# Low parts of 24 weight tiles by accumulating transfers, norms by logarithm and exponential, and one PSUM pool

## The chip, the cores and the metric

The kernel runs on one core of a Trainium2 chip. The metric is the device time of one execution in microseconds (us), and the figure of a kernel is the median of its runs. The engines are called as in the profile: PE (TensorE, matrix products), DVE (VectorE), ACT (ScalarE), POOL (GpSimd) and SP (SyncE, which issues the transfers). PSUM, the memory that PE writes its products to, has eight banks.

## The reference

Two layers of an encoder run over 1024 prompt tokens and 32 sample tokens that share all weights, in fp32. Each layer is

```
x <- LN(alpha * x + mixer(x))          # in-projection, mixers, output projection w_out (1024 x 1024)
x <- LN(alpha * x + SwiGLU(x))         # (silu(x @ w1) * (x @ w3)) @ w2, hidden width 2816
x <- x + (p[i] @ W_ple) * sigmoid(x @ W_gate)
LN(x) = (x - mean) * rsqrt(var + 1e-5) * g + b
```

The mixers are pooling and a gated convolution in layer 0, and a spatial gate and a state space scan in layer 1. Nothing of them is touched by the change.

## The kernel before, in words

**Operands in two parts.** A matrix product in fp32 precision is made of three products of a reduced type (fp32r): the high part of the weight with the high part of the activation, the low part of the weight with the high part, and the high part of the weight with the low one (lines 314 to 316). So each weight tile is split: a transfer on SP's queue brings it into a buffer `raw` (there are 2), ACT copies it with rounding into the high part (line 93), and DVE subtracts the high part from `raw` to make the low part (line 94). The pairs (`w`) have 4 places. A tile is 128 x 1024 in the projections (a "unit") and 128 x 512 in most of the SwiGLU. `Weights` runs 4 tiles ahead of the products that use them, so that loads and splits are issued in the middle of other work.

**The order.** The tokens are worked in three pieces c of 384, 384 and 288 columns in the projections, and in two halves of 528 in the SwiGLU. The matrix products of the SwiGLU use a fast scheme of seven block products (and, for some blocks, a second level of seven inside them) instead of eight; their results are added on DVE into the areas `s_all` and `c_all` (the tile names of the profile). The instructions are first recorded, then a scheduler puts them in each engine's order; it knows the dependences and durations of its own model, and the order on an engine is then fixed.

**Stages of a layer.** The mixer, the output projection with its norm, the first tiles of `w1_` and `w3_` (`f` = 0 and 1, as units), the rest of the up products (`up`, lines 1236 and 1153), the down products (`final`, line 1448), the second norm, and the embedding.

**Up and final.** `up` works in a PSUM pool with three tiles q of two banks and two tiles of one bank, `ia` and `ib`. `within` (called for the second level) makes seven block products in `ia` and `ib`: `one` issues six matmuls of 264 columns into one bank, and `to` reads that bank with ACT (line 1162, a copy) or DVE (line 1164, an addition). Each product that follows in the same bank waits for the reader of the one before. `final` then opens another pool, with four tiles q.

**The norm.** Per piece, `norm` makes the mean and variance by a product with ones (`ms`), then 1/sqrt(var) in steps that are put among other work by `defer`: a root on ACT (line 1685), a reciprocal on DVE (line 1690), a square on ACT (line 1691) and one step of refinement (lines 1697 to 1703). Between them, `minus` subtracts the mean from two of eight slices at a time (line 1673). `pieces` then scales (line 1709 on DVE, line 1711 on ACT) and splits the result into high parts (line 411, ACT) and low parts (line 412, DVE), two slices at a time, four times. The first tiles of `w1_` and `w3_` on piece 0 need these parts.

Of the kernel before, what the change touches and what calls it, by code (L numbers as in the profile page):

```python
# [9 lines left out]
AF = mybir.ActivationFunctionType  # L10
# [44 lines left out]
class Weights:  # L55
# [35 lines left out]
    def split(self, t, x):  # L91
# [2 lines left out]
        self.nc.vector.tensor_tensor(lo, x, hi.bitcast(F32), op=ALU.subtract)  # L94
        return hi, lo

    def sub(self, a, b, op=ALU.subtract):
        t = self.temp(a.shape[1])
        self.nc.vector.tensor_tensor(t, a, b, op=op)  # L99
        return t  # L100

    def _make(self, order):
        for kind, key, src in order:
            if kind == "steps":
                yield from src()
            elif kind == "unit":
                raw = self.raw(src)
                yield key, 2, self.split(self.place()[:, :, :src.shape[1]], raw)
            elif kind == "set":
                yield from self._set(key, *src)  # L110
            elif kind == "22":
                yield key, 1, self.split(self.half(), self.raw(src[1][:, 512:1024]))
            else:

                r0, r1 = (self.raw(v) for v in src)
                a11, a12, a21, a22 = (r[:, h * 512:(h + 1) * 512] for r in (r0, r1) for h in range(2))
                own = lambda x: (key, 1, self.split(self.half(), x))
                if kind != "sums":
                    yield own(a11)
                    yield own(a12)  # L120
                s1 = self.sub(a21, a22, ALU.add)
                s2 = self.sub(s1, a11)
                if kind == "own":
                    yield own(self.sub(a12, s2))
                    continue
                yield own(s2)
                if kind == "all":
                    yield own(s1)
                yield own(self.sub(a11, a21))
                if kind == "sums":  # L130
                    yield own(s1)
                    continue
                yield own(self.sub(a12, s2))
                yield own(a22)
# [150 lines left out]
class Kernel:  # L285
# [50 lines left out]
    def build(self):  # L336
        nc, tc, a = self.nc, self.tc, self.a
        with ExitStack() as ctx:
# [44 lines left out]
            for layer in range(2):  # L383
                if layer == 0:
                    self.layer0_mixer(self.x, xraw)
                    mp.close()
                else:
                    self.layer1_mixer(self.x)
                with ExitStack() as stack:
                    self.hp = stack.enter_context(tc.tile_pool(name=f"h{layer}", bufs=1, reuse_waits="tile"))  # L390
                    self.w.temps, self.w.temp_bufs = self.hp, 5
                    self.tail(layer)
                    self.tp = stack.enter_context(tc.tile_pool(name=f"t{layer}", bufs=1, reuse_waits="tile"))
                    with tc.tile_pool(name=f"psu{layer}", bufs=1, space=PSUM, reuse_waits="tile") as self.psum:
                        self.psum_bufs = {"q": 3, "ia": 1, "ib": 1}
                        self.up(layer)
                    self.psum = stack.enter_context(
                        tc.tile_pool(name=f"psb{layer}", bufs=1, space=PSUM, reuse_waits="tile")
                    )
                    self.psum_bufs = {"q": 4}  # L400
                    self.final(layer)
                    self.embed(layer)

# [736 lines left out]
    def within(self, layer, j, g):  # L1140


        nc, q, d, x = self.nc, TH // 2, self.sh, self.inside[j]
        m, t = {2: (0, 0), 4: (1, 0)}[j]
        (w,) = self.w.get(("in", layer, g, j))

        def bank(tag):
            return self.bank(tag)[:, :q]

        def one(ps, i, add):  # L1150
            for k in range(2):
                for c, (p, r) in enumerate(((0, 0), (1, 0), (0, 1))):
                    nc.tensor.matmul(  # L1153
                        ps, w[i][p][:, k * P:(k + 1) * P], x[i][r][:, k, :],
                        start=not add and k == 0 and c == 0, stop=k == 1 and c == 2, skip_group_check=add,
                    )
            self.passed(6 * q)

        def to(a, b, ps, new=False):
            o = d[a][:, m, t * TH + b * q:t * TH + (b + 1) * q]  # L1160
            if new:
                nc.scalar.activation(o, ps, AF.Copy)
            else:
                nc.vector.tensor_tensor(o, o, ps, op=ALU.add)

        u = bank("ia")
        one(u, 1, False)
        to(0, 0, u)
        v = bank("ib")
        one(v, 2, False)  # L1170
        to(0, 0, v)
        yield
        v = bank("ib")
        one(v, 5, False)
        to(1, 1, v, True)
        one(u, 6, True)
        to(0, 1, u)
        yield
        one(v, 3, True)
        to(0, 1, v)  # L1180
        one(u, 7, True)
        to(1, 1, u)
        yield
        one(u, 4, True)
        to(1, 0, u, True)
        yield
# [460 lines left out]
    def norm(self, ln, c, S, acc, x, n, done, wait=LN_A, rows=None):  # L1647
# [33 lines left out]
        def second():  # L1681
            ps, cut = average(S[1])
            nc.vector.tensor_tensor(cut(var), ps, cut(tmp), op=ALU.subtract)
            nc.vector.tensor_scalar(out=var, in0=var, scalar1=0.0, scalar2=EPS, op0=ALU.max, op1=ALU.add)
            nc.scalar.activation(tmp, var, AF.Sqrt)
            minus(0)
            self.defer(LN_B, third)

        def third():
            nc.vector.reciprocal(inv, tmp)  # L1690
            nc.scalar.activation(tmp, inv, AF.Square)
            minus(2)
            self.defer(LN_B, fourth)

        def fourth():

            nc.vector.tensor_tensor(tmp, tmp, var, op=ALU.mult)
            nc.scalar.activation(tmp, tmp, AF.Copy, scale=-0.5, bias=1.5)
            minus(4)
            self.defer(LN_B, fifth)  # L1700

        def fifth():
            nc.vector.tensor_tensor(inv, inv, tmp, op=ALU.mult)
            pieces(0)

        def pieces(k):
            ks = slice(k, k + 2)
            z = acc[:, ks, :]
            nc.vector.tensor_tensor(z, z, inv.unsqueeze(1).to_broadcast([P, 2, n]), op=ALU.mult)
            for kk in (k, k + 1):  # L1710
                nc.scalar.activation(
                    acc[:, kk, :], acc[:, kk, :], AF.Identity,
                    scale=self.ln[:, ln, 0, kk:kk + 1], bias=self.ln[:, ln, 1, kk:kk + 1],
                )
            if k == 0:
                minus(6)
            self.split(x, ks, z)
            done[c] += 1
            if k + 2 < KD:
                self.defer(LN_D if rows else LN_C, lambda: pieces(k + 2))  # L1720
# [118 lines left out]
```

## Time and profile before

| | |
|---|---|
| median of 3 runs | 2300.8 us (2297.95 to 2302.07) |
| profiled execution, its time | 2300.83 us |
| its span in the trace | 2298.6 us |
| PE busy | 2270.4 us (99%) |
| DVE, ACT, POOL busy | 1736.9, 1060.7, 32.5 us |
| mean TensorE clock granted | 0.996 |

The span runs from the first to the last recorded instruction; about 2.2 us of the execution's time lie outside it. A matmul's row in the trace has a start and a modelled end; as they are pipelined, the distance from start to start is what one costs. A timeline row with "x24" covers 24 instructions that follow one another. A bracket at the end of a row tells how long the engine sat idle before it and what released it.

### The profile page before, as it was taken

How to read it: one execution, taken by the hardware profiler on the slowest of the kernel's cores; microseconds unless marked ns; L12 is line 12 of the kernel's file. 1: busy time of each engine (PE TensorE's matmuls, PEld its weight loads, DVE VectorE, ACT ScalarE, POOL GpSimd, SP SyncE). 2: the span in 40 equal slices, each digit the busy share in tenths (PEclk: the TensorE clock that was granted, in tenths of full speed). 3: DMA queues.
4: the chain of work that ended last, by engine and by line, in shares of the span. 5: the costliest groups of instructions: out<-in, count | busy, mean ns of one | idle time of the engine just before them, and what ended most of it. 6: DMA issues, size and time to landing. Idle time of an engine off the chain costs nothing.

```text
span 2298.6 us, 41143 instructions
## 1 busy us (share of the span) xinstructions
PE 2270.4 (99%) x17183; PEld 2236.8 (97%) x17183; DVE 1736.9 (76%) x2820; ACT 1060.7 (46%) x1783; POOL 32.5 (1%) x40
## 2 busy tenths in 40 slices
PE   9999999999999999999999999999999999999998
PEld 8999989999999999999999989999999999999998
DVE  8755798977776788896656774898977776888893
ACT  5432464434443443584542662464444443434581
POOL 0000000000000000000000120000000000000000
PEclk9999999999999999999999999999999999999999
DMA  4113133333334632034211222142332335631132
GB/s 143 55 56 113 56 140 102 107 116 107 107 116 162 255 121 70 28 102 139 84 38 57 102 67 72 38 154 96 123 111 94 112 107 204 256 106 42 47 105 91
DMA packets 96478, 241.46 MB, mean 105 GB/s; under 512 B 12092, under 2 KB 21508, under 8 KB 94244
## 3 DMA queue, kind: packets, MB, share of 16 engines
q1 hardware_dynamic: 95524, 238.15, 30.5%
q8 instruction: 134, 2.20, 0.4%
q10 hardware_dynamic: 768, 0.68, 0.1%
q14 instruction: 52, 0.43, 0.1%
HBM read 196.99 MB, written 41.81 MB: 104 GB/s over the span
## 4 chain that ended last, share of the span: by engine, by line
PE 88%; DVE 7%; DMA 2%; ACT 2%; issue 1%; SPq 0%; POOL 0%; POOLq 0%; ACTq 0%
PE q L1236 28%; PE q L1448 20%; PE q L1576 8%; PE mm L314 6%; PE mm L315 6%; PE mm L316 6%; PE ia L1153 4%; PE ib L1153 3%; PE q L1555 2%; DVE bf L99 1%; PE mm L727 1%; PE mm L728 1%; PE mm L729 1%; DVE w L94 1%; DMA raw<-w 1%; PE ms L863 1%
## 5 line engine op out<-in xcount | busy, mean ns | idle before, releaser
L1448 PE MATMUL q<-w 128*128 128x264 f32 x3696 | 459.1, 286 | 4.3 <-DVE c_all L1254 2.2
L1448 PEld LDWEIGHTS q<-w 128*128 128x128 f32 x3696 | 457.8, 189 | 4.9 <-ACT w L93 4.7
L93 ACT ACTIVATE w<-bf 128x512 fp32r<-128x512 f32 (+1 forms) x314 | 184.5, 626 | 190.2 <-issue 69.1
L94 DVE TENSOR_TENSOR w<-raw,w 128x512 fp32r<-128x512 f32 (+2 forms) x182 | 171.2, 946 | 97.7 <-ACT w L93 97.5
L94 DVE TENSOR_TENSOR w<-bf,w 128x512 fp32r<-128x512 f32 (+1 forms) x314 | 207.0, 687 | 37.7 <-ACT w L93 37.3
L93 ACT ACTIVATE w<-raw 128x512 fp32r<-128x512 f32 (+2 forms) x182 | 149.1, 828 | 163.9 <-PE mm L316 75.2
L314 PE MATMUL mm<-xhgate,w 128*128 128x384 f32 (+1 forms) x576 | 188.6, 327 | 4.7 <-ACT xhgate L411 4.7
L1236 PE MATMUL q<-xhin,w 128*128 128x264 f32 x1152 | 188.3, 285 | 0.6 <-ACT u L481 0.6
L316 PE MATMUL mm<-xlgate,w 128*128 128x384 f32 (+1 forms) x576 | 186.6, 325 | 0.8 <-DVE xlgate L412 0.8
L315 PE MATMUL mm<-xhgate,w 128*128 128x384 f32 (+1 forms) x576 | 187.1, 325 | 0.0
L1576 PE MATMUL q<-xhgate,w 128*128 128x264 f32 x1024 | 167.1, 285 | 0.0
L1236 PEld LDWEIGHTS q<-xhin,w 128*128 128x128 f32 x1152 | 159.5, 188 | 1.5 <-ACT u L481 0.8
L1576 PEld LDWEIGHTS q<-xhgate,w 128*128 128x128 f32 x1024 | 142.0, 188 | 0.3
L314 PE MATMUL mm<-xhin,w 128*128 128x384 f32 (+1 forms) x384 | 127.4, 332 | 7.8 <-ACT xhin L411 5.6
L315 PE MATMUL mm<-xhin,w 128*128 128x384 f32 (+1 forms) x384 | 126.1, 329 | 0.6 <-DVE w L94 0.6
L316 PE MATMUL mm<-xlin,w 128*128 128x384 f32 (+1 forms) x384 | 125.7, 329 | 0.1
L1236 PE MATMUL q<-xhgate,w 128*128 128x264 f32 x768 | 125.3, 285 | 0.3 <-ACT xhgate L1204 0.2
L1236 PE MATMUL q<-t3sum,w 128*128 128x264 f32 x960 | 124.3, 285 | 0.0
L1236 PE MATMUL q<-t1sum,w 128*128 128x264 f32 x960 | 124.0, 285 | 0.0
L1236 PE MATMUL q<-t2sum,w 128*128 128x264 f32 x960 | 123.6, 284 | 0.0
L1236 PEld LDWEIGHTS q<-t1sum,w 128*128 128x128 f32 x960 | 120.3, 189 | 0.0
L1236 PEld LDWEIGHTS q<-t3sum,w 128*128 128x128 f32 x960 | 120.0, 189 | 0.0
(431 smaller groups left out, 4801.9 us busy)
## 6 DMA issues: line engine op xcount, KB each, us to landing
raw<-w SPq DMA_DIRECT2D x116, 512.0 KB, 3.7
hidden<-c_all SPq DMA_DIRECT2D x72, 264.0 KB, 2.1
rawx<-w SPq DMA_DIRECT2D x64, 256.0 KB, 2.9
raw<-w_gate SPq DMA_DIRECT2D x32, 512.0 KB, 3.6
raw<-w_in SPq DMA_DIRECT2D x16, 512.0 KB, 3.8
raw<-w_out SPq DMA_DIRECT2D x16, 512.0 KB, 3.5
xhdown<-hidden SPq DMA_DIRECT2D x12, 528.0 KB, 13.6
resid<-stream SPq DMA_DIRECT2D x4, 1056.0 KB, 4.9
```

The costliest lines, as they stand in the source:

```text
L93: self.nc.scalar.activation(hi, x, AF.Copy)
L94: self.nc.vector.tensor_tensor(lo, x, hi.bitcast(F32), op=ALU.subtract)
L99: self.nc.vector.tensor_tensor(t, a, b, op=op)
L314: nc.tensor.matmul(ps, wh, xh, start=first, stop=False)
L315: nc.tensor.matmul(ps, wl, xh, start=False, stop=False)
L316: nc.tensor.matmul(ps, wh, xl, start=False, stop=last)
L727: nc.tensor.matmul(o, xh, hi[:, s], start=k == 0, stop=False)
L1153: nc.tensor.matmul(ps, w[i][p][:, k * P:(k + 1) * P], x[i][r][:, k, :], start=not add and k == 0 and c == 0, stop=k == 1 and c == 2, skip_ ...
L1236: nc.tensor.matmul(ps[:, a, :TH // 2], w[q][:, ks], x[r][:, k, a * TH // 2:(a + 1) * TH // 2], start=not add and k == 0 and j == 0, stop=k ...
L1448: nc.tensor.matmul(ps[m][:, a, :TH // 2], v[q][:, ms], x[r][:, a * TH // 2:(a + 1) * TH // 2], start=j == 0 and n == 0, stop=j == NG - 1 a ...
L1555: nc.tensor.matmul(ps[:, b, :TH // 2], w[q][:, o:o + P], pe[k][r][:, t * TH + b * TH // 2:t * TH + (b + 1) * TH // 2], start=k == 0 and i ...
L1576: nc.tensor.matmul(ps[:, b, :TH // 2], w[q][:, ks], token_half((self.xh, self.xl), k, t, b)[r], start=k == 0 and i == 0, stop=k == KD - 1 ...
```

## The change

Three edits. First, for the units of `w_out`, `w1_` and `w3_` (24 tiles: eight of `w_out` and four of `w1_`/`w3_` in each layer), `split_dma` takes the place of `split`: the high part is made as before, ACT writes minus the high part into the low part's place by a second copy, and a transfer issued by POOL adds `raw` to that place. No DVE instruction is left in it. Second, the norm makes 1/sqrt(var) as exp(-0.5 ln(var)) with three ACT instructions in a row; the reciprocal and one deferred step are gone, and the subtractions of the mean are spread over other steps. Third, the pool of `up` and that of `final` are one, with four tiles q; `within` takes one q and uses its two banks.

```diff
+    def split_dma(self, t, x):
+        hi, lo = t[:, 0, :], t[:, 1, :]
+        self.nc.scalar.activation(hi, x, AF.Copy)
+        self.nc.scalar.activation(lo, x, AF.Copy, scale=-1.0)
+        self.nc.gpsimd.dma_start(out=lo, in_=x, accum_op=ALU.add)
+        return hi, lo
...
                 raw = self.raw(src)
-                yield key, 2, self.split(self.place()[:, :, :src.shape[1]], raw)
+                split = self.split_dma if key[0].startswith(("w_out", "w1_", "w3_")) else self.split
+                yield key, 2, split(self.place()[:, :, :src.shape[1]], raw)
...
-                    with tc.tile_pool(name=f"psu{layer}", bufs=1, space=PSUM, reuse_waits="tile") as self.psum:
-                        self.psum_bufs = {"q": 3, "ia": 1, "ib": 1}
-                        self.up(layer)
                     self.psum = stack.enter_context(
                         tc.tile_pool(name=f"psb{layer}", bufs=1, space=PSUM, reuse_waits="tile")
                     )
                     self.psum_bufs = {"q": 4}
+                    self.up(layer)
                     self.final(layer)
...
-        u = bank("ia")
+        ps = self.quads()
+        u, v = (ps[:, a, :q] for a in range(2))
         one(u, 1, False)
         to(0, 0, u)
-        v = bank("ib")
         one(v, 2, False)
         to(0, 0, v)
         yield
-        v = bank("ib")
         one(v, 5, False)
...
-            nc.scalar.activation(tmp, var, AF.Sqrt)
+            nc.scalar.activation(tmp, var, AF.Ln)
+            nc.scalar.activation(inv, tmp, AF.Exp, scale=-0.5)
+            nc.scalar.activation(tmp, inv, AF.Square)
             minus(0)
             self.defer(LN_B, third)
 
         def third():
-            nc.vector.reciprocal(inv, tmp)
-            nc.scalar.activation(tmp, inv, AF.Square)
+
+            nc.vector.tensor_tensor(tmp, tmp, var, op=ALU.mult)
+            nc.scalar.activation(tmp, tmp, AF.Copy, scale=-0.5, bias=1.5)
             minus(2)
             self.defer(LN_B, fourth)
 
         def fourth():
-
-            nc.vector.tensor_tensor(tmp, tmp, var, op=ALU.mult)
-            nc.scalar.activation(tmp, tmp, AF.Copy, scale=-0.5, bias=1.5)
-            minus(4)
-            self.defer(LN_B, fifth)
-
-        def fifth():
             nc.vector.tensor_tensor(inv, inv, tmp, op=ALU.mult)
             pieces(0)
...
-            if k == 0:
-                minus(6)
+            if k < 4:
+                minus(k + 4)
```

The scheduler makes new orders of this. Three places follow; the number behind an underscore tells buffers apart, and a bracket names what an instruction waits for (DMASW is the completion of a transfer issued by POOL).

**PE, third unit of the output projection of layer 0** (`mm48` and `mm49` are two output tiles of piece 0, `w83` the unit). Before:

```order
L314 MATMUL mm48_2062<-xhin_63,w83_1988 128x384 [waits Activation_49]
L314 MATMUL mm49_2076<-xhin_63,w83_1988 128x384
L315 MATMUL mm48_2062<-xhin_63,w83_1988 128x384 [waits DVE_49]
L316 MATMUL mm48_2062<-xlin_64,w83_1988 128x384
```

Now:

```order
L323 MATMUL mm50_2096<-xhin_63,w85_1996 128x384 [waits DVE_49,Activation_49]
L323 MATMUL mm51_2110<-xhin_63,w85_1996 128x384 [waits DVE_49]
L323 MATMUL mm52_2124<-xhin_63,w79_1843 128x384 [waits DVE_49]
L324 MATMUL mm52_2124<-xhin_63,w79_1843 128x384
L325 MATMUL mm52_2124<-xlin_64,w79_1843 128x384
...
L323 MATMUL mm53_2138<-xhin_63,w79_1843 128x384 [waits DVE_49]
L324 MATMUL mm48_2068<-xhin_63,w83_1990 128x384 [waits DMASW2_49]
L325 MATMUL mm48_2068<-xlin_64,w83_1990 128x384
```

Work on the fourth unit (`w85`) and on the first one again (`w79`, for piece 1) now stands between the third unit's high product and its low one, which waits for a transfer of POOL instead of DVE.

**PE, one second-level block in `up`** (six matmuls make one product of `within`). Before:

```order
L1153 MATMUL ia136_4512<-xhin_63,w194_4358 128x264 [waits Activation_49]
L1153 MATMUL ia136_4512<-xhin_63,w194_4358 128x264
...
L1153 MATMUL ib137_4520<-xhin_63,w194_4358 128x264 x2
L1153 MATMUL ib137_4520<-xlin_64,w194_4358 128x264
L1236 MATMUL q138_4535<-t1sum0_3226,w197_4441 128x264 [waits DVE_49]
...
L1153 MATMUL ib139_4561<-inner0_3945,w195_4361 128x264 [waits DVE_49]
L1153 MATMUL ib139_4561<-inner0_3945,w195_4361 128x264 x5
L1153 MATMUL ia136_4512<-inner0_3945,w195_4361 128x264 x6
```

Now:

```order
L1157 MATMUL q134_4522<-xhin_63,w194_4368 128x264 [waits DVE_49]
...
L1239 MATMUL q135_4544<-t1sum0_3238,w197_4451 128x264 x17
L1157 MATMUL q134_4522<-xhin_63,w194_4368 128x264 [waits DVE_49]
...
L1239 MATMUL q135_4544<-t1sum0_3238,w197_4451 128x264 x4
L1239 MATMUL q133_4485<-t2sum0_3239,w197_4451 128x264 x4
L1157 MATMUL q134_4522<-inner0_3957,w195_4371 128x264 [waits DVE_49]
L1157 MATMUL q134_4522<-inner0_3957,w195_4371 128x264 x5
L1239 MATMUL q133_4485<-t2sum0_3239,w197_4451 128x264 x4
L1157 MATMUL q134_4522<-inner0_3957,w195_4371 128x264 [waits Activation_49]
```

Before, two products of a block stood next to each other, one in each bank, and only the first of them waited. Now both banks belong to one tile, each product waits for the reader of the product before it, and 4 to 20 other matmuls stand between them.

**PE, from `up` to `final`** (`w370` and `w371` are the first two operands of `final`). Before:

```order
L1448 MATMUL q210_7873<-w370_7779 128x264 [waits DVE_49,PE_49,Activation_49]
L1448 MATMUL q210_7873<-w370_7779 128x264 x5
L1448 MATMUL q210_7873<-w371_7784 128x264 [waits Activation_49]
L1448 MATMUL q210_7873<-w371_7784 128x264 x5
```

Now:

```order
L1451 MATMUL q178_7849<-w370_7759 128x264 [waits PE_49,Activation_49]
L1451 MATMUL q178_7849<-w370_7759 128x264
L1451 MATMUL q178_7849<-w370_7759 128x264 [waits DVE_49]
...
L1451 MATMUL q178_7849<-w371_7764 128x264 x3
L1451 MATMUL q179_7850<-w370_7759 128x264 [waits PE_49]
```

The first product of `final` takes a PSUM tile that was free for some time, where it had to wait for the whole pool of `up` before.

More of the change, by code (lines that the diff above doesn't have):

```diff
@@ L1145, in within @@
         (w,) = self.w.get(("in", layer, g, j))
-        def bank(tag):
-            return self.bank(tag)[:, :q]
         def one(ps, i, add):
```

## The prediction

> **What bounds the kernel now.** I read the shares of the engines, the chain of waits, the waits of PE, and the busy time by stage.
>
> ```profile
> PE 2270.4 (99%) x17183; PEld 2236.8 (97%) x17183; DVE 1736.9 (76%) x2820; ACT 1060.7 (46%) x1783; POOL 32.5 (1%) x40
> PE 88%; DVE 7%; DMA 2%; ACT 2%; issue 1%; SPq 0%; POOL 0%; POOLq 0%; ACTq 0%
> PE mm L314 <- ACT xhin L411: 5.6, 2, 4.4
> PE mm L314 <- ACT xhgate L411: 4.7, 2, 4.4
> PE mm L314 <- ACT w L93: 2.2, 2, 1.8
> PE q L1448 <- DVE c_all L1254: 2.2, 1, 2.2
> PE q L1448 <- ACT w L93: 2.1, 1, 2.1
> PE mm L315 <- DVE w L94: 0.6, 1, 0.6
> 380.00:741.00 361.00, 361.00 (x2953) 360.55 (x2953) 270.02 (x483) 155.16 (x275) 0.00 (x0) 1.00 0.33 114
> ```
>
> PE works 99% of the span, at the full clock, and the change takes no matmul from it. So nearly all of the DVE work that goes is hidden work, and only PE's idle time, 28 us in all, can be won back. The waits (us in total, times, longest) name where it can be: the first SwiGLU tiles of both layers, 5.6 and 4.7, wait for the high parts of the normed piece; the last wait before `final`, 2.2 and 2.1; and the weights of the output projection, most of a microsecond. The last row is `up` of layer 0: 361.00 us of PE work in 361. There is nothing to win there, and a good deal to lose.
>
> **The work itself.** Prices of what goes and comes:
>
> ```profile
> 195.98 1.06 ACT L93 ACTIVATE w<-raw 128x1024 fp32r<-128x1024 f32 x1 [5.31 <-DMA raw<-w_out]
> 197.07 1.23 DVE L94 TENSOR_TENSOR w<-raw,w 128x1024 fp32r<-128x1024 f32 x1 [1.91 <-ACT w L93]
> L1690 DVE RECIPROCAL dg<-S x6: 1942/2541/2552, 267.3 to 1514.7; 128x384 f32<-128x384 f32 x4, 128x288 f32<-128x288 f32 x2
> L1690 DVE RECIPROCAL t2down<-t2down x4: 3442/3444/3445, 978.6 to 2215.6; 128x528 f32<-128x528 f32 x4
> L1685 ACT ACT_TABLE_LOAD  x8: 1283/1283/1283, 265.4 to 2212.9; - x8
> raw<-w_out SPq DMA_DIRECT2D x16, 512.0 KB, 3.5
> xhdown<-hidden SPq DMA_DIRECT2D x12, 528.0 KB, 13.6
> ```
>
> DVE loses 24 x 1.23 = 29.5 us of subtractions and 4 x 2.54 + 2 x 1.94 + 4 x 3.44 = 27.8 us of reciprocals. ACT gains 24 x 1.06 = 25.4 us of copies, and 12 table loads, because the built program has one ahead of each logarithm and another ahead of each exponential: 12 x 1.283 = 15.4 us. On busy time alone this is 57 us off DVE and 41 us onto ACT at 46%: nothing on PE. What counts is when things come.
>
> The Trainium skill ("ScalarE: Activation LUTs", What ACT_TABLE_LOAD costs) gives some 2.66 us for a switch, 1283 ns for the load and 1380 ns for a drain; by that the loads would cost ACT 32 us. The load in the trace agrees, 1283 ns; at 265.4 us it starts, and the root behind it starts at 266.7, so no drain follows it here, and I take 1.283.
>
> The unknown is L, from POOL's issue of an adding transfer until its data have landed; the trace has none. Its nearest rows are 3.5 us for a load of the same 512 KB and 13.6 us for one of 528 KB behind others. An addition must also read its destination; I take 5, a load and half as much again, nearer to the short row since these are issued singly, and keep 3.5 and 8 for the range (13.6 only if they queue behind a whole area's loads).
>
> The Trainium skill ("DMA: Bandwidth & Descriptors", Anatomy of one DMA) gives 2.0 us + bytes/436e3 for a transfer issued by POOL, 3.2 us for this size, and with it every term in L below would be at its lower bound. "SBUF — State Buffer" (the "DVE blocks DMA" trap) says that such a transfer gets no descriptors while certain DVE operations run, 620 ns becoming 3100; that would be the third rival below. No run here shows either.
>
> **Output projection, units three and four of layer 0.** These come late, since their loads stand behind the residual's.
>
> ```profile
> 183.51 15.14 SPq L84 DMA_DIRECT2D raw<-w_out  x3
> 197.09 0.62 PE L314 MATMUL mm<-xhin,w 128*128 128x384 f32 x2 [0.42 <-ACT w L93]
> 198.35 0.44 PE L315 MATMUL mm<-xhin,w 128*128 128x384 f32 x1 [0.64 <-DVE w L94]
> 198.63 0.34 PE L316 MATMUL mm<-xlin,w 128*128 128x384 f32 x1
> 198.80 0.34 PE L314 MATMUL mm<-xhin,w 128*128 128x384 f32 x1
> ```
>
> ACT has the third unit's high part at 197.04 as before. Its second copy ends at 198.1, and the low part lands at 198.1 + L: 203.1, where DVE ended at 198.3. The new order puts 17 other matmuls, 17 x 0.176 (two starts of the rows) = 3.0 us, into the gap, but the first of them needs the fourth unit's high part, which ACT copied at 199.35 before and still does: a stall of some 1.2 us ahead of them. Behind it the loss is 1.2 + max(0, L - 3.7): **2.5 us** at 5; 1.2 at 3.5; 5.5 at 8.
>
> **The other units.** Here the two `raw` buffers matter: a buffer is now free only when the addition has landed, and SP's next load waits in its queue, with those behind it.
>
> ```profile
> 226.80 1.06 ACT L93 ACTIVATE w<-raw 128x1024 fp32r<-128x1024 f32 x1 [27.45 <-PE mm L316]
> 236.07 0.34 PE L314 MATMUL mm<-xhin,w 128*128 128x384 f32 x1
> ```
>
> Unit five is copied from 226.80 (its place is freed by PE) to 228.9 and lands at 228.9 + L; then unit seven is loaded (3.5), copied twice (2.1) and added: 234.5 + 2L. PE begins with unit five's products at 236.07, and needs unit seven 48 x 0.176 = 8.5 us later, at 244.5. So at 5 us it just fits: **0** in either layer; at 8 it is 6 us late, twice (less what other work covers).
>
> **First tiles of the SwiGLU.**
>
> ```profile
> 281.14 0.85 ACT L411 ACTIVATE xhin<-stream 128x768 fp32r<-128x768 f32 x1
> 288.72 2.54 DVE L1690 RECIPROCAL dg<-S 128x384 f32<-128x384 f32 x1
> 297.53 0.83 ACT L411 ACTIVATE xhin<-stream 128x768 fp32r<-128x768 f32 x1
> 298.41 0.69 PE L314 MATMUL mm<-xhin,w 128*128 128x384 f32 x1 [4.44 <-ACT xhin L411]
> 298.90 0.52 PE L315 MATMUL mm<-xhin,w 128*128 128x384 f32 x1
> 299.22 0.52 PE L314 MATMUL mm<-xhin,w 128*128 128x384 f32 x1
> 302.42 0.68 PE L1664 MATMUL ms<-S,cst 128*128 128x288 f32 x1
> ```
>
> Before, the first high part of piece 0 is ready at 282.0 and the fourth at 298.4, held up by DVE, whose own work for piece 1, the reciprocal above among it, stands in between. Now the first comes 2.5 (reciprocal) + 2 (one deferred step) earlier, at 277.5. Between it and the fourth ACT has four copies of weights (4.2), six scalings at 0.65 (3.9), three high parts (2.5), squares and averages (2.2), and piece 1's logarithm, exponential and square with two loads (4.1): 16.9, so the fourth is there at 294.4, 4 us earlier. But the gain is not PE's: the new order has 30 matmuls behind that part which before ran ahead of it. They take 30 x 0.176 = 5.3, or 7.2 when the first 13 run at 0.32 (298.90 to 299.22) after the idle time: 299.7 to 301.6. The next weight, third of these tiles, is copied behind all this until 297.7 and its low part lands at 302.7 with L = 5, where PE stood at the same point at 302.42 before. **+0.3** (-2 at L = 3.5 to +3.3 at 8); in layer 1 the same sum gives **0** (-1.5 to +3).
>
> **From `up` to `final`.**
>
> ```profile
> 738.83 2.23 PE L1236 MATMUL q<-t3sum,w 128*128 128x264 f32 x17
> 743.26 1.49 PE L1448 MATMUL q<-w 128*128 128x264 f32 x7 [2.20 <-DVE c_all L1254]
> 741.80 1.31 DVE L1254 TENSOR_TENSOR c_all<-c_all,q 128x528 f32<-128x528 f32 x2
> ```
>
> PE stops at 741.06 and waits until DVE has read the last two results, since a new pool needs the old one empty. In one pool the first product takes a tile long free and needs only its operands (ready between 739 and 741.3). The second product, 12 matmuls or 1.5 us later, needs a bank that DVE frees at 743.1. Of 2.2 us I count **-1.6** in each layer, **-3.3** in all (0 to -4.4).
>
> **`up` itself.** Each layer has 16 blocks of `within`.
>
> ```profile
> 397.67 3.09 PE L1236 MATMUL q<-t3sum,w 128*128 128x264 f32 x24
> 400.60 0.64 PE L1236 MATMUL q<-xhin,w 128*128 128x264 f32 x4
> 447.90 0.40 PE L1153 MATMUL ib<-xhin,w 128*128 128x264 f32 x2
> 449.92 0.42 DVE L1164 TENSOR_TENSOR s_all<-s_all,ia 128x264 f32<-128x264 f32 x1
> L1162 ACT ACTIVATE c_all<-ia x32: 366/371/393, 441.8 to 1939.1; 128x264 f32<-128x264 f32 x32
> L93 ACT ACTIVATE w<-rawx x16: 1047/1047/1053, 432.5 to 1909.5; 128x1024 fp32r<-128x1024 f32 x16
> ```
>
> A matmul costs (400.60 - 397.67)/24 = 0.122. At 447.90 the product in `ia` was done, its addition started at 449.92: DVE comes 2 us late, and before, 24 matmuls (2.9 us) stood between two products in a bank. Now each of the six later products waits for the reader of the one before, behind 4 to 20 matmuls, 0.5 to 2.4 us. The scheduler has moved the readers up, so a usual turn is a read of 0.37 to 0.42 and 0.25 for the way to and from it, some 0.65. Against the tightest cover, 4 matmuls (0.49), that is 0.15 late; where ACT's copy stands behind a `w<-rawx` of 1.05, more. I take 0.2 a block, **+6.4** for 32 (0 if all are covered; 1 us each, +32, if one reader a block stands behind such a copy).
>
> Sum: 2.5 + 0 + 0.3 + 0 - 3.3 + 6.4 = 5.9; half of the last term is what I can least vouch for, and I settle at +3: 2300.83 + 3 = **2303.8**. The profiled execution's 2300.83 is the median, so nothing is to be shifted.
>
> **The rivals.** *The waits in `up` are all covered.* The kernel is faster. For it: DVE is busy 270 of 361 us there and the scheduler ordered by these waits; against it: the 4-matmul cover. Then -3.3 to -4.4 at the switch, -2 and -1.5 at the first tiles, +1.2 at the projection: 5.6 to 6.7 below, about 2295. *Each block stalls about 1 us* for a reader that stands behind one long instruction on its in-order engine (DVE's 1.2 us split, ACT's 1.05 us copy); it decides once the mean delay passes the 0.5 us cover. Slower by 32 less the 0.5 gained elsewhere: up to 2332, or 2322 at 0.7 a block. *The additions are slow*, L = 8 or more: 5.5 + 2 x 5.8 + 3.3 + 3 - 3.3 + 6.4 = +26.5, some 2320 to 2327; for it, the 13.6 us row and the destination's second pass; against it, POOL's queue has nothing else. *PE still waits before `final`*, since its first operands are made on ACT and DVE late: only the 3.3 is lost, 2307, a part of the forecast's range.
>
> **How the numbers follow.** Small change around my sum, 2297 to 2310: 0.47. Waits covered: 0.25. Blocks stall: 0.17. Slow additions: 0.11. The range 2293 to 2322 takes in the first rival and the near ends of the two with a loss, and leaves out some 0.2. A difference under 0.2% (4.6 us) can't be told here from none. Below 2296.2: most of the first rival and a little of the forecast, 0.25. Above 2305.4: the two with a loss, 0.28, and a quarter of the forecast's case, 0.12: 0.40. Between: 0.35.
>
> **What would show it.** Right: waits of PE in `up` on the second-level products (line 1157) of 0.1 to 0.3 us each, 3 to 10 us in all; the wait ahead of `final` down to under 1 us; the adding transfers at 4 to 6 us; the fourth high part near 294 with no gain behind it. Wrong: a sum of those waits under 2 or over 15 us, transfers past 6 us with waits of PE on them at units seven and eight, or first tiles that end 3 us earlier than before.

## The result, and the profile after

The changed kernel takes 2333.5 us (median; 2329.3 to 2336.0) against 2301.4 before: the ratio is 1.014, with a 95% interval of 1.0123 to 1.0157. It is slower by 32 us, where +3 was forecast with a range up to 2322. Its profiled execution took 2329.32 us with a span of 2327.6, 29 us above the span before.

The busy time of the engines and the transfers that POOL issues (count, KB, median us to landing) on the page of the changed kernel:

```profile
PE 2290.2 (98%) x17183; PEld 2242.3 (96%) x17183; DVE 1693.2 (73%) x2786; ACT 1105.3 (47%) x1829; POOL 53.4 (2%) x64
...
w<-raw POOLq DMA_DIRECT2D x24, 512.0 KB, 5.3
```

Its longest waits of PE (us in total, times, longest):

```profile
PE mm L324 <- DMA w<-raw: 8.5, 5, 2.8
PE mm L323 <- ACT w L100: 5.7, 2, 4.8
PE mm L323 <- ACT xhgate L418: 3.8, 2, 2.9
PE q L1239 <- DVE s_all L1257: 2.9, 2, 1.7
PE ms L1667 <- DVE S L1647: 2.0, 1, 2.0
...
PE mm L323 <- ACT xhin L418: 0.9, 1, 0.9
```

And the adding transfers, from POOL's issue to landing:

```profile
DMA to landing us min/median/max: 4.5/5.3/11.4
```

DVE's busy time fell by 44 us and ACT's rose by 45, and the kernel's time followed neither. The same 17183 matmuls keep PE busy 20 us longer, and its idle time grew by 9. So two things happened. The listed waits have moved: the wait for the normed pieces (`xhin`, `xhgate`) fell from 10.3 to 4.7 us, the 4.3 us ahead of `final` are gone, and waits for POOL's transfers and for the output projection's weights came instead. The rest is in no row of this list, since it consists of stalls too short to be listed. The stages show where:

```profile
390.00:760.00 370.00, 367.54 (x2932) 360.28 (x2931) 271.76 (x480) 156.88 (x274) 0.00 (x0) 1.00 0.32 113
1600.00:1970.00 370.00, 368.32 (x2941) 361.50 (x2941) 272.03 (x481) 155.98 (x273) 0.00 (x0) 1.00 0.32 110
```

These are the two `up` stages: 2932 matmuls in 370 us, where 2953 ran in 361 before. PE's clock is 1.00 in both.

I took the distance from start to start of all matmuls, less the median of their size (0.122 us for 264 columns, 0.175 for 384), and summed it between the same matmuls of both kernels. Of the 29 us, the second-level products of `up` cost 18.6 and other waits in `up` 2.7, and the switch to `final` gives 6.2 back. The output projections cost 10.8 in layer 0 and 5.6 in layer 1, and the first SwiGLU tiles give 1.3 and 0.8 back. The beginning of the program gives 2.4 back, and the rest costs 2.2. These are sums of one execution each; that of the changed kernel was the fastest of its four.

A part of these losses is in no wait. In or just behind some waits of PE the granted clock fell to one half for 3.4, 6.8 or 10.2 us, and a matmul of 384 columns then cost 0.32 us where 0.175 is usual. The longest such stretch of the changed kernel begins in PE's longest wait, which ends at 199.09 (stretch, length, PE busy and matmuls, granted clock, busy share of the DMA engines, GB/s):

```profile
196.70:206.90 10.20, 6.92 (x20) 0.50 0.59 113
```

Not every wait of this kind had one: ahead of `final` of the kernel before, the wait of 2.2 us in layer 0 had 3.4 us at half the clock behind it, and that of 2.1 us in layer 1 had none. So a stage of a single execution is uncertain by 1 to 2 us.

### The profile page after: what moved, and what is told of

The parts are those of the page before. It is cut to its first block, busy times and chain, and to the rows that moved or that the text cites. A ratio compares the mean times of both kernels' runs of the same rounds, so it can differ in the third digit from the quotient of the medians.

```text
span 2327.6 us, 41270 instructions
## 1 busy us (share of the span) xinstructions
PE 2290.2 (98%) x17183; PEld 2242.3 (96%) x17183; DVE 1693.2 (73%) x2786; ACT 1105.3 (47%) x1829; POOL 53.4 (2%) x64
## 4 chain that ended last, share of the span: by engine, by line
PE 80%; DVE 8%; ACT 5%; DMA 5%; issue 2%; POOL 0%; SPq 0%; POOLq 0%; ACTq 0%; DVEq 0%
PE q L1239 26%; PE q L1451 20%; PE q L1579 8%; PE q L1157 8%; PE mm L325 4%; PE mm L323 4%; PE mm L324 4%; DVE bf L107 2%; DMA raw<-w 2%; DMA raw<-w_out 1%; DVE w L94 1%; PE mm L734 1%; PE mm L735 1%; DMA w<-raw 1%; PE mm L736 1%
## 5 line engine op out<-in xcount | busy, mean ns | idle before, releaser
L94 DVE TENSOR_TENSOR w<-raw,w 128x512 fp32r<-128x512 f32 (+2 forms) x158 | 142.2, 904 | 66.6 <-ACT w L93 66.5
L93 ACT ACTIVATE w<-raw 128x512 fp32r<-128x512 f32 (+2 forms) x158 | 123.6, 792 | 76.8 <-PE q L1239 51.2
L1239 PE MATMUL q<-t2sum,w 128*128 128x264 f32 x960 | 131.3, 284 | 0.0
L1239 PE MATMUL q<-t1sum,w 128*128 128x264 f32 x960 | 129.2, 285 | 0.0
L1239 PEld LDWEIGHTS q<-t2sum,w 128*128 128x128 f32 x960 | 122.8, 188 | 0.0
```

The lines of the kernel that those rows point to most:

```text
L93: self.nc.scalar.activation(hi, x, AF.Copy)
L1239: nc.tensor.matmul(ps[:, a, :TH // 2], w[q][:, ks], x[r][:, k, a * TH // 2:(a + 1) * TH // 2], start=not add and k == 0 and j == 0, stop=k ...
```

## The experiments

### Each part alone

The three parts were each built into the kernel before; the diffs are those of the change.

**The adding transfers.** 

> Only the low parts of the 24 units by POOL's adding transfers; norms and PSUM pools as before. Theory 1 (each part pays for itself, as the waits of PE in the changed kernel's trace are placed): 8 to 15 us slower than before, with waits of PE on POOL's transfers at the first, third and seventh unit of the output projections and the third of the first SwiGLU tiles, 7 to 12 us in all, and up unchanged. Theory 2 (the transfers are covered; the changed kernel's waits there come from the orders that the three parts make together): within 3 us of before.

Measured: 2315.9 against 2300.9, ratio 1.0071 (1.0059 to 1.0084), 15 us slower. Theory 1, at the upper end of its range, with 13.0 us of waits on the transfers where it had 7 to 12. Its waits of PE:

```profile
PE mm L324 <- DMA w<-raw: 13.0, 6, 3.0
PE mm L323 <- ACT w L100: 6.2, 3, 4.8
```

**The norms.** 

> Only the norms with logarithm and exponential. Theory 1: 0 to 6 us faster, since the fourth high part of piece 0 comes about 4 us earlier in each layer and nothing else stands behind it. Theory 2 (the 12 table loads and the three ACT instructions in a row make ACT the chain of the pieces): 0 to 5 us slower, with the fourth high part no earlier than before.

Measured: 2304.0 against 2300.9, ratio 1.0015 (1.0007 to 1.0024), some 3 us slower. Theory 2 in the time, but not in its sign: the fourth high part of piece 0 was ready at 295.8 us, where it was 298.4 before.

**The pool.** 

> Only the one PSUM pool, with within in the two banks of one tile. Theory 1: 14 to 20 us slower; the second-level products (line 1148 or near) cost some 9 us a layer more, the wait ahead of final goes (-2 us a layer). Theory 2 (up is late because ACT or DVE carry other work of the change): 0 to 5 us faster, the gain of the switch alone.

Measured: 2312.4 against 2300.9, ratio 1.0056 (1.0044 to 1.0068), 11.5 us slower. Theory 1, a little under its range. The three add up to 29.7 of the 32 us, so each part pays mostly for itself, and each was a loss.

### The pool: who shares a tile

```diff
-        ps = self.quads()
-        u, v = (ps[:, a, :q] for a in range(2))
+        u, v = (self.quads()[:, 0, :q] for _ in range(2))
```

> The one pool, but within takes two tiles and uses one bank of each, so that two products no longer share a tile. Theory 1a (the loss is that a product waits for the reader of the other bank, because both belong to one tile): the cost of the second-level products falls from about 9 to under 3 us a layer, and the kernel is 12 us or more faster than with one tile, near before. Theory 1b (the loss is too few matmuls between a product and its reader, or too few free tiles): it stays within 6 us of the kernel with one tile, or is slower, with waits on other q tiles.

Measured: 2295.7 against 2300.9, ratio 0.9977 (0.9968 to 0.9985): 5 us faster than before, and 16.7 faster than with one tile. Theory 1a. The opposite experiment keeps the two pools and joins `ia` and `ib` into one tile:

```diff
-                        self.psum_bufs = {"q": 3, "ia": 1, "ib": 1}
+                        self.psum_bufs = {"q": 3, "i": 1}
...
-        u = bank("ia")
+        self.nbank += 1
+        ps = self.psum.tile([P, 2, 512], F32, tag="i", name=f"i{self.nbank}", bufs=1)
+        u, v = (ps[:, a, :q] for a in range(2))
...
-        v = bank("ib")
...
-        v = bank("ib")
```

> The kernel before with its two PSUM pools, but ia and ib made one tile of two banks, which within uses as the changed kernel does. Theory 1a (the loss in up is the shared tile alone): 15 to 19 us slower than before, with about 9 us a layer at the second-level products and the waits ahead of final as before. Theory 1c (it is within taking one of the four tiles that the rest of up would use): within 4 us of before, since the other three tiles are untouched here.

Measured: 2316.8 against 2300.9, ratio 1.0075 (1.006 to 1.009), 16 us. Theory 1a again: the tile alone does it, with the rest of the pool untouched. Summed as above, the second-level products lose 9.3 us a layer in the changed kernel and 9.0 to 9.7 in the two others with one tile; with two tiles they lose nothing that can be told. The largest group of these products shows it (busy us, mean ns of one), first the changed kernel, then the shared tile in two pools, then two tiles:

```profile
L1157 PE MATMUL q<-inner,w 128*128 128x264 f32 x576 | 92.7, 297 | 0.6 <-ACT c_all L1166 0.2
```

```profile
L1150 PE MATMUL i<-inner,w 128*128 128x264 f32 x576 | 92.5, 296 | 0.3
```

```profile
L1148 PE MATMUL q<-inner,w 128*128 128x264 f32 x576 | 80.9, 284 | 0.0
```

Almost none of it stands as idle time behind the bar; it is in the busy column. One such place in the timelines of PE and ACT of the changed kernel:

```profile
462.87 0.66 PE L1239 MATMUL q<-t2sum,w 128*128 128x264 f32 x4
463.52 1.00 PE L1157 MATMUL q<-inner,w 128*128 128x264 f32 x6
464.35 0.53 PE L1239 MATMUL q<-t2sum,w 128*128 128x264 f32 x3
463.07 0.39 ACT L1166 ACTIVATE c_all<-q 128x264 f32<-128x264 f32 x1 [0.61 <-PE q L1157]
```

The four matmuls of cover should take 0.49 us from start to start and take 0.65: the product behind them waits for ACT's copy of the other bank, which ends at 463.46. That wait of 0.16 is what I had forecast. But the six matmuls of the product then take 0.83 us instead of 0.73, with nothing more to wait for: the second of them starts 0.23 us behind the first, where 0.122 is usual. In each layer, 33 or 34 of the 112 products start more than 0.03 us late, 4.6 us in all, and in each of these the second matmul is late as well, by 0.10 to 0.11. The second matmul is late at 44 products a layer, 4.5 us in all, and at some of them the first came less than 0.03 late. So the waits are half of the 9.3 us, and the late second matmuls are the other half.

The two-tile form was also put into the whole change:

> The whole change with within in two tiles instead of two banks of one. Theory A (the shared tile's price is its own): 15 to 18 us faster than the whole change, so 14 to 17 us slower than before. Theory B (part of it is work that waits elsewhere for the transfers): under 12 us faster than the whole change.

Measured: 2315.6 against 2297.9 in that comparison, ratio 1.0075 (1.0061 to 1.0088); the whole change has 1.014. So it gains 15 to 18 us there as well: theory A, though with 17.7 over before it ends a little above the 14 to 17 named.

### The adding transfers: landing, copies, or POOL

```diff
-        self.nc.gpsimd.dma_start(out=lo, in_=x, accum_op=ALU.add)
```

> As the kernel with the adding transfers alone, but without the transfers: ACT's second copy stays, the addition is left out, so the low parts are minus the rounded weight and the products of the low parts have no meaning. Theory A (the loss of 15 us is the time until the addition lands, in which PE lacks the low part and SP lacks a raw buffer): it falls to 4 us or less over before. Theory B (the loss is ACT's second copies, 1.06 us each ahead of other work on ACT): it stays at 10 us or more.

Measured: 2290.4 against 2300.9, ratio 0.996 (0.9946 to 0.9973): 10 us *faster* than before. Theory A. ACT's 24 copies are not what makes the loss, and between this kernel and the one with transfers lie 25 us, not 15. In the trace, whose execution was the slowest of the four and 5 us faster than before, the gain is at the first SwiGLU tiles: they cost 6.8 us less in layer 0 and 5.8 in layer 1, while `up` costs 9 more. The waits for the high parts of the normed pieces, 10.3 us before, are nearly gone:

```profile
PE mm L322 <- ACT xhin L419: 0.6, 1, 0.6
PE mm L322 <- ACT xhgate L419: 0.6, 1, 0.6
```

DVE is rid of 24 subtractions here, and before it was busy for all of the 24 us from 280 to 304, in this stage of layer 0. Whether that or the new order of the instructions brings the gain isn't separated. Another part, 1.5 us, is in the order on SP: here the loads of the third and fourth units stand ahead of the residual's on SP, as raw buffers are free early. First SP's issues in this kernel, then in the changed one:

```profile
174.89 2.87 SPq L84 DMA_DIRECT2D raw<-w_out  x2
177.82 4.40 SPq L426 DMA_DIRECT2D stream<-xT  x3
```

```profile
177.18 7.26 SPq L425 DMA_DIRECT2D stream<-xT  x3
184.55 23.77 SPq L84 DMA_DIRECT2D raw<-w_out  x4
```

How long the residual's three loads (`stream<-xT`) took until they landed, before, in the changed kernel, and without the transfers (min, median, max):

```profile
DMA to landing us min/median/max: 7.6/11.1/13.7
```

```profile
DMA to landing us min/median/max: 10.4/14.2/18.1
```

```profile
DMA to landing us min/median/max: 7.7/9.4/11.2
```

The two additions of the first units run at the same time as these loads, and the loads land later with them. So the third unit, whose load is behind, came later too, and PE, which got there 2.4 us earlier than before, waited for its high part, not only for the low one:

```profile
199.09 1.01 PE L323 MATMUL mm<-xhin,w 128*128 128x384 f32 x2 [4.76 <-ACT w L100]
200.99 1.33 PE L323 MATMUL mm<-xhin,w 128*128 128x384 f32 x3 [0.89 <-ACT w L100]
```

The DMA engines were shared in that time. In the changed kernel (stretch, length, granted clock, busy share of the DMA engines, GB/s), with additions under way until 183.5:

```profile
177.00:180.00 3.00, 1.00 0.99 166
180.00:185.00 5.00, 1.00 1.04 257
185.00:190.00 5.00, 1.00 1.05 368
```

The engines are full in all three stretches, but move less with the additions among the loads. No run takes the additions alone out of this order.

Next, POOL subtracts instead:

```diff
-        self.nc.scalar.activation(lo, x, AF.Copy, scale=-1.0)
-        self.nc.gpsimd.dma_start(out=lo, in_=x, accum_op=ALU.add)
+        self.nc.gpsimd.tensor_tensor(lo, x, hi.bitcast(F32), op=ALU.subtract)
```

> In the kernel before, the low parts of the 24 units are subtracted by POOL instead of DVE, without transfers and without ACT's second copies. Theory A (what costs with the adding transfers is the 5.3 us until they land, in which the buffer is held and PE lacks the low part): POOL takes some 2.3 us (an estimate, twice the 1.165 us of its 128x512 rows), so the loss falls from 15 to under 4 us, or becomes a gain of up to 6, since DVE is freed as with the transfers. Theory B (these low parts must not come later than DVE makes them at all, or POOL and DVE slow each other): 6 us slower than before or more.

Measured: 2307.8 against 2301.7, ratio 1.0026 (1.0014 to 1.0039), 6 us slower: at the bound of theory B. POOL's subtraction takes 2574 ns against DVE's 1220:

```profile
L101 POOL TENSOR_TENSOR w<-raw,w 128x1024 fp32r<-128x1024 f32 x24 | 61.7, 2574 | 349.1 <-ACT w L100 349.0
```

But none of PE's listed waits is for POOL's parts. Two of the three longest, 4.8 and 3.5 us in all, are for the low parts of the normed pieces, which DVE makes, and there POOL holds DVE up. In layer 0, on POOL, DVE and PE:

```profile
292.85 5.88 POOL L101 TENSOR_TENSOR w<-raw,w 128x1024 fp32r<-128x1024 f32 x2 [7.41 <-ACT w L100]
292.51 0.95 DVE L420 TENSOR_TENSOR xlin<-stream,xhin 128x768 fp32r<-128x768 f32 x1
296.51 3.03 DVE L420 TENSOR_TENSOR xlin<-stream,xhin 128x768 fp32r<-128x768 f32 x1
299.60 0.44 PE L324 MATMUL mm<-xlin,w 128*128 128x384 f32 x1 [2.23 <-DVE xlin L420]
```

The second of POOL's two subtractions runs from 296.37 to 298.73, and DVE's beside it takes 3.03 us, where the same subtraction takes 0.95 otherwise. Of the DVE instructions beside POOL's 24 subtractions, 12 are longer than others of their kind by 1.4 to 2.2 us each, some 25 us in all. So POOL and DVE do slow each other, as theory B has it in its second half. By the sums of the trace the output projections cost 3.0 us more than before, `up` 5.6 more (3.7 of them waits for weights from ACT) and the first SwiGLU tiles 1.0 less; why `up` is slower stays open. So the 6 us are no price of a later low part alone, and they don't tell what a freed DVE is worth: it was freed of 24 subtractions and held up by nearly as much.

> One PSUM pool with within in two tiles, and POOL's subtractions for the 24 units; norms as before. If the two add up: 5 us faster than before plus what POOL's subtractions alone give. If they meet (the stages are apart, so I don't expect it), less than half of that.

Measured: 2299.2 against 2301.7, ratio 0.9993 (0.9984 to 1.0002): no difference to before; the two roughly add.

Where the loss sits:

```diff
-                split = self.split_dma if key[0].startswith(("w_out", "w1_", "w3_")) else self.split
+                split = self.split_dma if key[0].startswith("w_out") else self.split
```

> The adding transfers for the 16 units of the output projections alone; the 8 tiles of w1_ and w3_ as before. If the loss of 15 us sits at the projections' third and seventh units and their first ones (theory A): 9 to 13 us slower. If it sits at the first tiles of the SwiGLU (theory B): under 5 us slower.

Measured: 2316.6 against 2301.7, ratio 1.0066 (1.0049 to 1.0084), as much as with all 24. Theory A, beyond its upper end: all of it is in the output projections (11.5 us in layer 0 and 6.6 in layer 1 by the sums of the trace). With all 24, the first SwiGLU tiles even come out 2.9 and 1.6 us better than before: they wait for transfers, but the wait for the normed pieces, 10.3 us before, is not among the longest any more. At the seventh unit of layer 0 of the changed kernel, on POOL, SP, ACT and PE:

```profile
234.46 0.87 POOL L102 DMA_DIRECT2D w<-raw  x1 [31.33 <-ACT w L101]
239.40 4.18 SPq L84 DMA_DIRECT2D raw<-w_out  x2
245.97 1.06 ACT L100 ACTIVATE w<-raw 128x1024 fp32r<-128x1024 f32 x1 [8.41 <-DMA raw<-w_out]
248.33 0.86 POOL L102 DMA_DIRECT2D w<-raw  x1 [9.56 <-ACT w L101]
252.91 0.45 PE L324 MATMUL mm<-xhin,w 128*128 128x384 f32 x1 [2.78 <-DMA w<-raw]
```

and at the first units of layer 1:

```profile
1417.28 0.44 PE L324 MATMUL mm<-xhgate,w 128*128 128x384 f32 x1 [2.09 <-DMA w<-raw]
```

The fifth unit is handed to POOL at 234.46; its `raw` buffer is loaded again from 239.40 for the seventh unit, which ACT gets at 245.97; handed over at 248.33, it reaches PE at 252.91. From the first hand-over to the second it is 13.9 us: one addition (4.9), one load (6.6) and two copies.

### The norms: what costs in them

```diff
-            minus(4)
             self.defer(LN_B, fifth)
...
-            if k == 0:
-                minus(6)
+            if k < 4:
+                minus(k + 4)
```

> Only the subtractions of the mean are spread as in the change; root, reciprocal and all steps as before. If ACT's table loads and the logarithm and exponential are what makes the changed norm 3 us slower (theory A): faster than before by 1 to 4 us, since the pieces meet less DVE work ahead of them. If the spreading is what costs (theory B): 2 to 5 us slower.

Measured: 2300.9 against 2300.9, ratio 1.0005 (0.9996 to 1.0013): no difference. Neither theory; the spreading by itself makes no difference that can be told. The other half:

```diff
         def third():
             minus(2)
+            minus(4)
             self.defer(LN_B, fourth)
...
-            if k < 4:
-                minus(k + 4)
+            if k == 0:
+                minus(6)
```

> Only logarithm, exponential and square with one deferred step fewer; the subtractions of the mean all come before or with the first piece as before. Theory A (ACT's table loads are the cost): 2 to 5 us slower, as with the whole norm changed. Theory B (the spreading costs): 0 to 4 us faster.

Measured: 2308.5 against 2300.9, ratio 1.0033 (1.0021 to 1.0046), 7.6 us slower. Theory A, more than it said. With logarithm and exponential the spreading does help, by some 4 us (7.6 against 3.2). In the timeline of ACT with the norms alone changed, in the middle of piece 0:

```profile
285.39 1.29 ACT L1707 ACTIVATE stream<-stream,prm 128x384 f32<-128x384 f32 x2
286.70 1.28 ACT L1685 ACT_TABLE_LOAD   x1
288.00 0.53 ACT L1685 ACTIVATE S<-S 128x384 f32<-128x384 f32 x1
288.43 0.83 ACT L411 ACTIVATE xhin<-stream 128x768 fp32r<-128x768 f32 x1
289.28 1.28 ACT L1686 ACT_TABLE_LOAD   x1
290.57 0.53 ACT L1686 ACTIVATE dg<-S 128x384 f32<-128x384 f32 x1
```

Piece 1's norm puts two table loads between the scalings of piece 0 and its high parts, and ACT has no gap. To separate the loads from the chain:

```diff
-            nc.scalar.activation(tmp, var, AF.Ln)
-            nc.scalar.activation(inv, tmp, AF.Exp, scale=-0.5)
+            nc.scalar.activation(tmp, var, AF.Copy)
+            nc.scalar.activation(inv, tmp, AF.Copy, scale=-0.05, bias=0.7)
```

> The changed norm alone, but the logarithm and the exponential are copies with a scale and an offset: the same three ACT instructions in the same chain, no table loads for them (34 loads in the built program, against 59 with the changed norm and 47 before), and norms of wrong size. Theory A (the loads, 1.283 us each in the middle of ACT's chain of scalings and high parts, make the changed norm's loss): 2 to 8 us faster than before. Theory B (the chain's length or the order of the steps makes it): 1 to 4 us slower than before, as with logarithm and exponential.

Measured: 2292.5 against 2302.9, ratio 0.9954 (0.994 to 0.9968), 10 us faster. Theory A: the same three instructions without loads turn the loss into a gain. (They also drop later loads, as the function that was in the table before stays in it.) A form with the right values and one function:

```diff
-            nc.scalar.activation(tmp, var, AF.Ln)
-            nc.scalar.activation(inv, tmp, AF.Exp, scale=-0.5)
+            nc.scalar.activation(inv, var, AF.Abs_reciprocal_sqrt)
```

> The changed norm with one ACT function that gives the reciprocal of the root, in place of logarithm and exponential: one table load for a norm as before (47 in the built program), and no reciprocal on DVE. Theory A (table loads in ACT's chain make the changed norm's loss; without any, it was 10 us faster than before): 3 to 8 us faster than before. Theory B (the gain without loads came from the wrong sizes or the order alone): within 3 us of before.

Measured: 2290.3 against 2297.9, ratio 0.9956 (0.9942 to 0.9969), 8 to 10 us faster. Theory A, by its median of 7.7. By the sums of the trace the gain is at the first SwiGLU tiles, 5.1 us in layer 0 and 4.8 in layer 1, where logarithm and exponential lose 1.6 and gain 0.3. The loads of the norm before, with logarithm and exponential, and with the one function (count, busy us and mean ns):

```profile
L1685 ACT ACT_TABLE_LOAD x8 | 10.3, 1283 | 5.6 <-DVE S L1684 3.2 <-DVE t3down L1684 2.3
```

```profile
L1685 ACT ACT_TABLE_LOAD x10 | 12.8, 1283 | 6.3 <-DVE S L1684 3.2 <-DVE t3down L1684 2.9
L1686 ACT ACT_TABLE_LOAD x10 | 12.8, 1283 | 0.2
```

```profile
L1685 ACT ACT_TABLE_LOAD x8 | 10.3, 1283 | 0.1
```

### A version that beats both

> One PSUM pool with within in two tiles, and the norm with one load; low parts by DVE as before. If the two add: 5 us and what the norm with one load gains, 8 to 13 us faster than before. If they meet: no more than the better of the two.

Measured: 2286.1 against 2297.9, ratio 0.9948 (0.9935 to 0.9961), about 12 us faster than before and 47 faster than the changed kernel. The two gains add, at the low end of what their medians alone give (5 and 8).

## Why the prediction was wrong, point by point

- **That PE's waits decide, not busy time:** right as far as shown: DVE had 57 us less of instructions, and the kernel was slower. It doesn't follow that a freed DVE is worth nothing: without the transfers the first SwiGLU tiles gained 6.8 and 5.8 us.
- **`up` itself, +6.4, set to half of it:** the mechanism was right and its size was not; with the output projections this is where most of the error lies. The wait that I worked out (0.65 less a cover of 0.49) is there, 0.16. The waits of this kind come to 9.3 us in both layers, within the 3 to 10 that I named as a sign of being right. But the products lost 18.6 us, 0.58 in each of the 32 blocks. The step that failed is "0.2 a block": about two of a block's seven products wait, 0.29 in all, and the second matmul of a product comes late, mostly behind such a wait, another 0.29, for which I had no term. I then halved the term without a row that said so. The rival that gave 1 us a block was no nearer in its mechanism: it has one stall of 1 us, and no product started more than 0.35 us late.
- **From `up` to `final`, -3.3:** the mechanism was right, and the gain was larger than its bounds (0 to -4.4): 6.2 by the sums above, since the two waits are gone whole, and with them the 3.4 us at half the clock in layer 0. `final` follows without a gap; in the changed kernel's PE timeline the last product of `up` and the first of `final`, 24 matmuls or 2.91 us apart:

```profile
756.41 3.07 PE L1239 MATMUL q<-t3sum,w 128*128 128x264 f32 x24
759.32 2.87 PE L1451 MATMUL q<-w 128*128 128x264 f32 x22
```

- **L = 5 us:** right; 5.3 in the median. The Trainium skill ("DMA: Bandwidth & Descriptors", Anatomy of one DMA) gives 2.0 us + bytes/436e3, an estimate of 3.2 us for this size; the fastest of the 24 took 4.5, so the measurement decides against it for an addition within SBUF.
- **Units three and four, +2.5:** too small; it was 7.7. The waits there are 4.8 and 0.9, against 0.4 and 0.6 before, and the 10.2 us at half the clock behind the first of them cost some 3 more. The step that failed is that ACT has the high part "at 197.04 as before": the loads ahead of it took longer, the residual's last 18.1 us instead of 13.7. I had priced the transfers' latency and not what they do to the loads beside them, nor the clock behind a wait.
- **The other units, 0:** wrong. 2.8 us at the seventh unit of layer 0, 1.2 at that of layer 1, and 2.1 at the first of layer 1, where I had no term. With the clock behind them, these places cost 3.1, 1.5 and 4.1 us. The sum 234.5 + 2L took a load at 3.5 us, and this one took 6.6: from the hand-over of the fifth unit to that of the seventh it was 13.9, where my sum has 10.6 with L = 5. All of it came 5.6 us later than in my sum, but so did PE.
- **First SwiGLU tiles, +0.3 and 0:** right within the bounds, -1.3 and -0.8. Measured from the `ms` product of piece 0, its first and fourth high parts came 4.8 and 5.4 us earlier, where I had 4.5 and 4. The wait for them fell by half, and others took its place, 1.9 us for the third tile's transfer in layer 0 among them.
- **The norms, no term of their own:** wrong. I had costed 12 more loads at 15.4 us of an engine that is busy 46%, put two of them into the chain of the first SwiGLU tiles, and left the rest there. In the norm's stage ACT isn't half idle: from 280 to 304 us of the kernel with the norms alone changed it is busy 19.0 of 24 us and DVE 20.9 (16.0 and 24.0 before). The measured price of logarithm and exponential is 3 us with the other edits of the norm; without their loads the same steps gain 10.
- **The range and the chances:** 2333.5 is outside 2293 to 2322. My cases with a loss ended at 2332 and 2327 each, but I drew the range as if only one of them could come. Neither came as I had written it, as L stayed near 5 and no product waited for 1 us. Losses of like size came in the same two places by other ways, and the norms on top. So several terms were too small at once.

## What to carry to other kernels

Two banks of one PSUM tile were one thing to the waits of this kernel: give products that follow closely their own tiles, and count the waits of an engine that runs at 99%, since here they had a price beyond their length, in the matmul behind them or in the clock. An engine that is half idle over the whole span can be the bound of a stage, so a price on it has to be put into that stage: 20 table loads of 1.28 us in the norms, where there were 8, made the kernel 3 us slower although 27.8 us of reciprocals were gone. A transfer that takes the place of an instruction holds its buffers until it lands, and here the loads beside it landed later; that cost more than the engine time that it saved.

## What the runs showed of the hardware that was not expected

- After each wait of PE of more than 0.03 us ahead of a second-level product in the changed kernel, the product's second matmul started 0.10 to 0.11 us late, with nothing more to wait for; with places behind shorter waits there were 44 a layer, 4.5 us. The page books such time as busy.
- In or just behind some waits of PE (of 4.8 us in the changed kernel, of 2.2 before, but not of 2.1 before), the granted clock was 0.50 for 10.2 and 3.4 us.
- An addition by a transfer of 512 KB within SBUF took 4.5 us at least, 5.3 in the median and 11.4 at most, and the loads that ran beside two of them landed up to 4.4 us later (18.1 against 13.7). The DMA engines were full then (share 0.99 and 1.04) at 166 and 257 GB/s, and moved 368 GB/s when the additions were done (1.05).
- A logarithm followed by an exponential took a table load each, 20 in the norms; the Trainium skill ("ScalarE: Activation LUTs", Table sets: the hidden batching unit) has both in one set with one load, which no run here shows. No drain stood behind a load (286.70 + 1.28, next start 288.00).
- POOL's subtraction of 128x1024 took 2.57 us, 2.1 times DVE's, and 12 DVE instructions beside the 24 of them took 1.4 to 2.2 us longer than others of their kind (3.03 instead of 0.95 in the rows above).
